# Four engine queues held to the written order of a streaming-encoder trunk

## The chip, the cores and the metric

The kernel runs on one core of a Trainium2 chip. The metric is the device time of one execution in microseconds (us). Each compute engine (PE for matrix products, DVE, ACT, POOL) works off its own instruction queue, and SP issues nearly all transfers. Instructions of different engines wait for each other through semaphores.

## The reference

One layer over 2,048 tokens of width 1,024, followed by a final norm:

```python
h = rmsnorm(x, norm_g)
c_b, c_c, c_h, c_z, q, k, v, a_z = split(h @ w_in)          # 8 groups of 512 columns
y_c = c_b * causal_dwconv(c_c * c_h, conv_w, conv_b)        # 3 taps
# stick-breaking attention, 8 heads of 64:
z = q @ k.T / 8
rem = reverse exclusive cumsum of log_sigmoid(-z)           # over s < t
y_a = where(s < t, exp(log_sigmoid(z) + rem), 0) @ v
y = group_rmsnorm(concat(y_c, y_a)) * silu(concat(c_z, a_z))
x = x + y @ w_out
x = x + sigmoid(rmsnorm(x) @ w_pg + b_pg) * (p @ w_pe)
return rmsnorm(x, final_g)
```

All of it is in float32, and the outputs are float32.

## The kernel before

**Tiles.** x lies transposed, in four chunks of 512 tokens, which are worked off as c = 3, 2, 1, 0; the pair (3, 2) is called E and the pair (1, 0) L. A projection tile is 128 output columns by 512 tokens. Each factor is split into a high and a low part (`wh`/`wl` for weights, `hhh`/`hhl` for activations; ACT makes the high part, DVE or POOL the low part by a subtraction), and one k-step of 128 is three products on PE (L276, L277, L278). Eight k-steps fill one PSUM tile `pp`. There are two such tiles (tag `mm`), so PE may start the next tile but one only when the evacuation of a tile has run on DVE (L338 for q and k, L388 for gates, L725 and L824 in the last part).

**Attention.** It is worked off in units of (head, query chunk, key chunk). Each unit has four rows. `row_z` makes two matmuls (L527, L528) into one of two `z` tiles, from which ACT takes `s` (L530) and `b` (L532). `row_scan` makes a scan T over s on DVE (L546, L549), POOL copies its last column as the carry (L553), and b times T is taken on DVE or POOL (L555). PE transposes the result (L594), ACT and DVE split it into `ah` and `al` (L597, L602), and two matmuls multiply it by v into `av` (L565, L566), of which there is a single tile. When a head's last unit is through, ACT copies one half of `av` (`tmp`, L574) and DVE adds the other (`ya`, L575); only then is the `av` tile free for the next head.

**Through DRAM.** q, k and v go through DRAM. `evac_qk` takes a tile of q and k from PSUM (DVE L338), makes `sh` (ACT L339) and `sl` (POOL L340), and two steps later issues five stores on SP (L345). `fetch_units` issues the loads of `q` (L509), `kk` (L513) and `vv` (L515) on SP as soon as the stores are recorded as issued, and the four `z` rows of that unit follow in the attention's code.

**Interleaving.** The projections are generators, and `run` goes through them a k-step at a time. After each step it adds a rate to `owed` and pulls that many pieces from the attention's generator. `later` puts off a piece of work by some steps, and `tick` counts them. The order in which the Python code emits instructions is called the written order here. Between it and the queues stands the tile framework's scheduler, which lists each engine's instructions in an order of its own at compile time, with an estimate of what will be ready when.

**Names in the rows.** `gg28_3` is the gate tile of column block 28 and chunk 3; `r2_3` are the norm factors of y for chunk 3, written in code far behind but made from `rg`, which POOL makes (L445) after a power (L439); `rr` is a chunk's norm factor, which PE spreads by a transpose (`rT`, L188); `g3_4` is a tile of the last gate; `z24`, `z72`, `z96`, `z120`, `z144` are the first rows of their units.

Of the kernel before, what the change touches and what calls it, by code (L numbers as in the profile page):

```python
# [28 lines left out]
LAG = 1  # L29

AHEAD = 2


def build(tc, xt_d, pt_d, wst_d, wpe_d, cst_d, out_d):
# [5 lines left out]
    with ctx:  # L40
# [458 lines left out]
        def fetch_units(upto):  # L499

            while got[0] <= min(upto, len(units) - 1):
                n = got[0]
                h, qc, kc = units[n]
                if not all((h, c) in s for c in (qc, kc) for s in (have_qk, have_v)):
                    return
                if kc == qc:
                    q = [att.tile([P, CH], F32R, tag=f"q{i}", bufs=2, name=f"q{i}_{h}_{qc}") for i in (1, 2)]
                    for i in range(2):
                        nc.sync.dma_start(q[i].bitcast(F32),  # L509
                                          qk_d[h][qc][i:i + 2].rearrange("a p t -> (a p) t"))  # L510
                    Q[h, qc] = q
                K[n] = att.tile([P, CH], F32R, tag="kk", bufs=4, name=f"kk{h}_{qc}_{kc}")
                nc.sync.dma_start(K[n].bitcast(F32), qk_d[h][kc][3:5].rearrange("a p t -> (a p) t"))  # L513
                V[n] = att.tile([P, 4, P], F32R, tag="vv", bufs=5, name=f"vv{h}_{qc}_{kc}")
                nc.sync.dma_start(V[n].bitcast(F32).rearrange("p a b -> p (a b)"), v_d[h][kc])  # L515
                got[0] += 1
# [92 lines left out]
        def attention():  # L609

            rows, z = {}, {}
            total = 4 * len(units)
            slots = turns()

            def slot():
                nonlocal slots
                if next(slots, "end") == "end":
                    slots = turns()
                    return next(slots, "end") != "end"
                return True  # L620

            for r in range(total):
                n, j = divmod(r, 4)
                while r not in z:
                    fetch_units(n + AHEAD)
                    if got[0] > n:
                        z[r] = row_z(r)
                    else:
                        yield False
                if j == 0:  # L630
                    fetch_units(n + AHEAD)
                if r + 1 < total and got[0] > (r + 1) // 4:
                    z[r + 1] = row_z(r + 1)
                product_of_row = row_scan(r, *z[r])
                rows.setdefault(n, []).append(z.pop(r))
                yield True
                if j == LAG and n:
                    unit = rows.pop(n - 1)
                    tiles_in_line.extend((n - 1, unit, i) for i in range(4))
                if slot():  # L640
                    yield True
                product_of_row()
                if slot():
                    yield True
            unit = rows.pop(total // 4 - 1)
            tiles_in_line.extend((total // 4 - 1, unit, i) for i in range(4))
            while slot():
                yield True
            while behind:
                weigh(*behind.pop(0))  # L650
                yield True
# [238 lines left out]

        cE, cL = (3, 2), (1, 0)
        stream = attention()
        owed = [0.0]

        def pull():
            return next(stream, None)
# [233 lines left out]
```

## Time and profile before

| | |
|---|---|
| time, median of three runs (lowest, highest) | 1666.65 us (1658.98, 1668.19) |
| the profiled execution's own time | 1666.16 us |
| its span in the trace | 1664.4 us |
| mean granted clock of PE | 0.981 |
| busy: PE, DVE, ACT, POOL | 96%, 68%, 47%, 44% |
| transferred | 334 MB, 201 GB/s on average |

The busy share of PE counts matmuls whose ends are modelled, and it counts a matmul at the lower of the two clock levels (1.2 and 2.4 GHz; a granted clock of 1.00 in the tables is 2.4) as busy for longer. So the time that PE loses in a stretch has two parts: the idle time beside the busy time, and the share by which the granted clock lies under 1.00. The time of the run outside the span is 1.8 us.

### The profile page before, as it was taken

The page shows a single profiled execution, that of the slowest core. Times are in us where ns is not written, and L with a number is a line of the kernel's source. Part 1 is how long each engine was busy: PE and PEld are TensorE (multiplying, and loading weights), DVE is VectorE, ACT ScalarE, POOL GpSimd, SP SyncE. Part 2 cuts the span into 40 slices and gives each one's busy share as a digit, 9 for nine tenths or more (in the row PEclk, how much of TensorE's full clock was granted, in tenths as well). Part 3 has the DMA queues.
Part 4 walks back from the last instruction along what each step waited for, and adds up shares of the span by engine and source line. Part 5 has one row for each costly group of instructions (what it writes and reads, how often), then busy time and mean ns, then how long its engine had stood idle before and what let it go on. Part 6 is the DMA issues. An engine that isn't in the chain of part 4 may idle for free. (4 is left out here: it accounts for less than half of the span.)

```text
span 1664.4 us, 23193 instructions
## 1 busy us (share of the span) xinstructions
PE 1596.0 (96%) x7602; PEld 1289.8 (77%) x7602; DVE 1129.0 (68%) x1473; ACT 782.0 (47%) x1540; POOL 726.6 (44%) x711
## 2 busy tenths in 40 slices
PE   8899999999999999999999999998999999999996
PEld 6687878888878788888888888776767887777875
DVE  7475675856745767777787787789787987334544
ACT  4344453544424545454554444456555554223453
POOL 6434444454360423232433323587574444325541
PEclk9999999999999999999999999999899999999998
DMA  5766765748547646475753433478677856888832
GB/s 178 240 215 201 229 215 184 246 135 272 176 157 226 187 151 173 133 226 152 234 165 114 133 108 121 135 266 286 224 245 259 309 188 215 270 305 285 268 112 84
DMA packets 184712, 333.99 MB, mean 201 GB/s; under 512 B 21776, under 2 KB 22800, under 8 KB 184592
## 3 DMA queue, kind: packets, MB, share of 16 engines
q1 hardware_dynamic: 181712, 327.27, 61.0%
q10 hardware_dynamic: 2880, 5.24, 0.9%
q8 instruction: 60, 0.98, 0.3%
q14 instruction: 60, 0.49, 0.1%
HBM read 217.08 MB, written 115.34 MB: 200 GB/s over the span
## 5 line engine op out<-in xcount | busy, mean ns | idle before, releaser
L276 PE MATMUL pp<-hhh,wh 128*128 128x512 f32 x1008 | 408.5, 405 | 4.7 <-DVE gg L388 3.1
L277 PE MATMUL pp<-hhl,wh 128*128 128x512 f32 x1008 | 403.1, 400 | 3.1 <-DVE hhl L155 3.0
L278 PE MATMUL pp<-hhh,wl 128*128 128x512 f32 x1008 | 400.7, 398 | 0.0
L549 DVE TENSOR_TENSOR_SCAN T<-s,carry,small 128x513 f32<-128x513 f32 x192 | 282.4, 1471 | 111.4 <-ACT s L530 104.6
L530 ACT ACTIVATE s<-z 128x512 f32<-128x512 f32 (+1 forms) x320 | 172.0, 538 | 310.6 <-PE z L528 302.7
L555 POOL TENSOR_TENSOR b<-b,T 128x512 f32<-128x512 f32 (+2 forms) x160 | 177.0, 1106 | 172.3 <-DVE T L549 96.3
L263 POOL TENSOR_TENSOR wl<-wr,wh 128x512 fp32r<-128x512 f32 x126 | 178.2, 1414 | 131.2 <-ACT wh L262 117.9
L277 PEld LDWEIGHTS pp<-hhl,wh 128*128 128x128 f32 x1008 | 192.5, 191 | 43.6 <-DVE hhl L155 8.0
L276 PEld LDWEIGHTS pp<-hhh,wh 128*128 128x128 f32 x1008 | 193.0, 192 | 42.3 <-DVE gg L388 3.5
L278 PEld LDWEIGHTS pp<-hhh,wl 128*128 128x128 f32 x1008 | 192.5, 191 | 42.6
L602 DVE TENSOR_TENSOR al<-tp,ah 128x512 fp32r<-128x512 f32 (+1 forms) x320 | 191.5, 599 | 43.8 <-ACT ah L597 43.0
L597 ACT CAST ah<-tp 128x512 fp32r<-128x512 f32 (+1 forms) x320 | 168.3, 526 | 62.5 <-PE tp L594 58.4
L553 POOL COPY carry<-T 128x1 f32<-128x1 f32 x192 | 54.7, 286 | 322.5 <-DVE T L549 170.0
L594 PE MATMUL tp<-first,b 128*128 128x128 f32 x1088 | 174.3, 274 | 9.9 <-POOL b L555 6.2
L594 PEld LDWEIGHTS tp<-first,b 128*128 128x128 f32 x1088 | 137.5, 141 | 52.6 <-POOL b L555 8.2
L532 ACT ACTIVATE b<-z 128x512 f32<-128x512 f32 (+1 forms) x320 | 170.2, 532 | 0.0
L546 DVE TENSOR_TENSOR_SCAN T<-s,first 128x513 f32<-128x513 f32 (+3 forms) x128 | 118.4, 931 | 62.1 <-ACT s L530 61.9
L565 PE MATMUL av<-ah,vv 128*128 128x512 f32 (+1 forms) x320 | 140.5, 439 | 7.3 <-DVE ya L575 7.3
L555 DVE TENSOR_TENSOR b<-b,T 128x512 f32<-128x512 f32 (+1 forms) x160 | 125.9, 787 | 11.8 <-ACT wh L262 0.5
L527 PE MATMUL z<-kk,q 128*128 128x512 f32 (+1 forms) x320 | 120.6, 377 | 4.4 <-DMA kk<-qk_d 2.3
L262 ACT CAST wh<-wr 128x512 fp32r<-128x512 f32 x126 | 78.2, 622 | 96.8 <-DMA wr<-in_wst_dram 41.5
L566 PE MATMUL av<-al,vv 128*128 128x512 f32 (+1 forms) x320 | 118.7, 371 | 2.5 <-DVE al L602 2.5
(156 smaller groups left out, 2623.0 us busy)
## 6 DMA issues: line engine op xcount, KB each, us to landing
wr<-in_wst_dram SPq DMA_DIRECT2D x128, 256.0 KB, 3.0
wh<-wp_d SPq DMA_DIRECT2D x128, 256.0 KB, 3.3
wl<-wp_d SPq DMA_DIRECT2D x128, 256.0 KB, 3.6
wp_d<-wh SPq DMA_DIRECT2D x94, 256.0 KB, 3.5
wp_d<-wl SPq DMA_DIRECT2D x94, 256.0 KB, 3.6
kk<-qk_d SPq DMA_DIRECT2D x80, 256.0 KB, 4.5
vv<-v_d SPq DMA_DIRECT2D x80, 256.0 KB, 3.8
q<-qk_d SPq DMA_DIRECT2D x64, 256.0 KB, 4.3
```

The costliest lines, as they stand in the source:

```text
L263: nc.gpsimd.tensor_tensor(out=wl, in0=raw, in1=wh.bitcast(F32), op=ALU.subtract)
L276: nc.tensor.matmul(pp, wh[:, sl], hh, start=(kt == 0), stop=False)
L277: nc.tensor.matmul(pp, wh[:, sl], hl, start=False, stop=False)
L278: nc.tensor.matmul(pp, wl[:, sl], hh, start=False, stop=(kt == KT - 1))
L530: nc.scalar.activation(s[:, 1:w + 1], zp[:, 0:w], AF.Sigmoid, scale=-0.125)
L532: nc.scalar.activation(bt[:, 0:w], zp[:, 0:w], AF.Sigmoid, scale=0.125)
L549: nc.vector.tensor_tensor_scan(T[:, 0:w + 1], s[:, 0:w + 1], zeros.to_broadcast([P, w + 1]), carries[h, qc][:, j:j + 1], op0=ALU.mult, op1 ...
L555: return lambda: eng.tensor_tensor(out=bt[:, 0:w], in0=bt[:, 0:w], in1=T[:, 0:w], op=ALU.mult)
L565: nc.tensor.matmul(av[:, 0:w], v[:, kb], ah[:, 0:w], start=diag and kb == 3, stop=False)
L594: nc.tensor.transpose(tp[:, j * P:(j + 1) * P], bt[:, kb * P - k0:(kb + 1) * P - k0], ident)
L597: nc.scalar.copy(ah[:, 0:w], tp[:, 0:w])
L602: nc.vector.tensor_tensor(out=al[:, 0:w], in0=tp[:, 0:w], in1=ah[:, 0:w].bitcast(F32), op=ALU.subtract)
```

## The change

A new function goes through the instructions as they were written, after the whole kernel has been recorded, and ties each instruction of DVE, PE, ACT and POOL to the one written before it on the same engine. The tie is an ordering for the scheduler, with no semaphore. SP is not in the list. Beside that, `owed` begins at -5 rather than 0, so the attention's pieces stand five pulls later among the projection steps, from the start on. No instruction is added or removed on a compute engine.

```diff
--- before.py
+++ after.py
@@ -29,6 +29,19 @@
 LAG = 1
 
 AHEAD = 2
+
+
+def in_line(tc, engines):
+
+    last = {}
+    for ins in list(tc.nc.cur_bb.bb.instructions):
+        if ins.engine in engines:
+            if ins.engine in last:
+                tc.add_manual_dep(
+                    ins, last[ins.engine].name,
+                    mybir.DependencyInfo(mybir.DependencyClass.NoSync, mybir.DependencyReason.DATA),
+                    reason="in_line")
+            last[ins.engine] = ins
 
 
 def build(tc, xt_d, pt_d, wst_d, wpe_d, cst_d, out_d):
@@ -890,7 +903,7 @@
 
         cE, cL = (3, 2), (1, 0)
         stream = attention()
-        owed = [0.0]
+        owed = [-5.0]
 
         def pull():
             return next(stream, None)
@@ -1124,6 +1137,7 @@
     args.append(nc.dram_tensor("out_0_dram", (4, KT, P, CH), F32, kind="ExternalOutput").ap())
     with tile.TileContext(nc) as tc:
         build(tc, *args)
+        in_line(tc, [mybir.EngineType.DVE, mybir.EngineType.PE, mybir.EngineType.Activation, mybir.EngineType.Pool])
     r = run_bass_kernel_spmd(nc, [arrays], core_ids=[0])
     out = r.results[0]["out_0_dram"]
     return np.ascontiguousarray(out.transpose(0, 3, 1, 2).reshape(SEQ, DM)[::-1]).reshape(1, SEQ, DM)
```

Below are three places in the queues; lines behind L31 have numbers greater by 13 in the changed file, so L276 to L278 there are L289 to L291, L527 is L540, L388 is L401, L549 is L562, L575 is L588 and L824 is L837.

PE, in the chunks L, where q and k of head 0 in chunk 1 (`pp16_1`) are ready and the rows of the first unit of the L chunks begin (`z96`). First before:

```order
L276 MATMUL pp17_1_5919<-hhh1_1_5508,wh17_68_5719 128x512
L277 MATMUL pp17_1_5919<-hhl1_1_5509,wh17_68_5719 128x512
L278 MATMUL pp17_1_5919<-hhh1_1_5508,wl17_68_5720 128x512
L276 MATMUL pp17_1_5919<-hhh1_2_5514,wh17_68_5719 128x512
L277 MATMUL pp17_1_5919<-hhl1_2_5515,wh17_68_5719 128x512
L527 MATMUL z96_5791<-kk0_1_1_5779,q1_0_1_5775 128x512
L528 MATMUL z96_5791<-kk0_1_1_5779,q2_0_1_5776 128x512
L527 MATMUL z97_5797<-kk0_1_1_5779,q1_0_1_5775 128x384
```

Then the same unit in the changed kernel:

```order
L289 MATMUL pp16_1_5718<-hhh1_7_5558,wh16_67_5700 128x512
L290 MATMUL pp16_1_5718<-hhl1_7_5559,wh16_67_5700 128x512
L291 MATMUL pp16_1_5718<-hhh1_7_5558,wl16_67_5701 128x512
L289 MATMUL pp16_0_5766<-hhh0_0_5597,wh16_66_5584 128x512
L290 MATMUL pp16_0_5766<-hhl0_0_5598,wh16_66_5584 128x512
L291 MATMUL pp16_0_5766<-hhh0_0_5597,wl16_66_5585 128x512
L540 MATMUL z96_5791<-kk0_1_1_5779,q1_0_1_5775 128x512
L541 MATMUL z96_5791<-kk0_1_1_5779,q2_0_1_5776 128x512
```

`z96` stood 59 rows behind the last product of `pp16_1` before (rows 2277 and 2337 of the queue, with products of `pp17_1` ahead of it); now three products lie between the two. In the same way `z24` and `z72` move up by 16 rows, `z120` by 10 and `z144` by 23. Of PE's 7,267 rows 6,572 keep their number. SP issues the loads of these units in nearly the same places of its own queue, behind the stores of the same tile.

DVE, at the gates of the attention's heads 0 and 1, chunk 3, before:

```order
L437 TENSOR_TENSOR gr3_2_5226<-gs3_2_5221,rr_460 128x32
L438 TENSOR_SCALAR gr3_2_5226<-gr3_2_5226 128x32
L602 TENSOR_TENSOR al22_1_5238<-tp22_1_5234,ah22_1_5237 128x256
L443 TENSOR_SCALAR gr7_3_5248<-gs7_3_5243 128x8
L668 CAST r2_3_11250<-rg_461 128x4x16
L669 TENSOR_TENSOR r2_3_11250<-rg_461,r2_3_11250 128x4x16
L388 TENSOR_TENSOR gg28_3_5262<-pp28_3_5180,rB3_738 128x512
L393 SCALAR_TENSOR_TENSOR gg28_3_5262<-gg28_3_5262,cst_439,sg28_3_5263 128x512
```

And now:

```order
L615 TENSOR_TENSOR al22_2_5195<-tp22_2_5190,ah22_2_5194 128x384
L562 SCALAR_TENSOR_TENSOR T95_5216<-s2_473,carry7_2_4918,small_448 128x513
L450 TENSOR_TENSOR gr3_2_5226<-gs3_2_5221,rr_460 128x32
L451 TENSOR_SCALAR gr3_2_5226<-gr3_2_5226 128x32
L456 TENSOR_SCALAR gr7_3_5248<-gs7_3_5243 128x8
L615 TENSOR_TENSOR al22_1_5238<-tp22_1_5234,ah22_1_5237 128x256
L401 TENSOR_TENSOR gg28_3_5262<-pp28_3_5180,rB3_738 128x512
L406 SCALAR_TENSOR_TENSOR gg28_3_5262<-gg28_3_5262,cst_439,sg28_3_5263 128x512
```

The two instructions that make `r2_3` stand 540 rows further behind now, at rows 981 and 982 of DVE's queue, and the evacuation of `gg28_3` no longer has them ahead of it.

DVE, in the last third, where the final gate (`g3_4`) runs beside the attention of heads 4 and 5 (`ya2_0`), before:

```order
L549 SCALAR_TENSOR_TENSOR T278_13107<-s2_473,carry5_0_12825,small_448 128x513
L555 TENSOR_TENSOR b278_13056<-b278_13056,T278_13107 128x512
L602 TENSOR_TENSOR al68_3_13072<-tp68_3_13066,ah68_3_13071 128x512
L686 TENSOR_TENSOR yt2_5_12964<-yt2_5_12964,gT2_5_13083 128x512
L824 TENSOR_TENSOR g3_4_13086<-px144_3_12942,rB7_12505 128x512
L549 SCALAR_TENSOR_TENSOR T279_13152<-s0_471,carry5_0_12825,small_448 128x513
L830 TENSOR_TENSOR g3_4_13086<-g3_4_13086,e3_4_13021 128x512
L693 TENSOR_TENSOR yhl2_5_13115<-yt2_5_12964,yhh2_5_13114 128x512
L602 TENSOR_TENSOR al68_2_13124<-tp68_2_13119,ah68_2_13123 128x384
L575 TENSOR_TENSOR ya2_0_13128<-av4_0_12407,tmp4_0_13129 64x512
```

And now:

```order
L562 SCALAR_TENSOR_TENSOR T277_13058<-s1_472,carry5_0_12825,small_448 128x513
L699 TENSOR_TENSOR yt2_5_12964<-yt2_5_12964,gT2_5_13083 128x512
L837 TENSOR_TENSOR g3_4_13086<-px144_3_12942,rB7_12505 128x512
L615 TENSOR_TENSOR al68_3_13072<-tp68_3_13066,ah68_3_13071 128x512
L562 SCALAR_TENSOR_TENSOR T278_13107<-s2_473,carry5_0_12825,small_448 128x513
L843 TENSOR_TENSOR g3_4_13086<-g3_4_13086,e3_4_13021 128x512
L588 TENSOR_TENSOR ya2_0_13128<-av4_0_12407,tmp4_0_13129 64x512
L568 TENSOR_TENSOR b278_13056<-b278_13056,T278_13107 128x512
L615 TENSOR_TENSOR al68_2_13124<-tp68_2_13119,ah68_2_13123 128x384
```

The evacuation of `g3_4` (L824, now L837) has moved ahead of two attention rows (`al68_3` and the scan `T278`) and the product of b278, and `ya2_0` (L575, now L588) ahead of that product, of `al68_2`, and of `yhl2_5`. On DVE, 206 of 1,470 rows keep their number; evacuations stand four to five rows earlier on average.

On ACT two changes of that kind lie near the start: `vo0_2`, `vo1_2` and `sh1_3` (L364, L339) stood behind the first unit's `s` and `b` rows and stand ahead of them now.

## Rows read from the trace of the kernel before

**Rows 1.** The page, part 1: busy time and share of each engine.

```profile
PE 1596.0 (96%) x7602; PEld 1289.8 (77%) x7602; DVE 1129.0 (68%) x1473; ACT 782.0 (47%) x1540; POOL 726.6 (44%) x711
```

**Rows 2.** Waits of PE: total us, times, longest us.

```profile
PE av L565 <- DVE ya L575: 7.3, 3, 3.3
...
PE rT L188 <- POOL rr L178: 5.4, 3, 2.8
...
PE gs L428 <- ACT sq L421: 3.5, 3, 2.7
PE pp L276 <- DVE gg L388: 3.1, 1, 3.1
```

**Rows 3.** Busy time by stretch; columns PE, PEld, DVE, ACT, POOL, granted clock, DMA.

```profile
240.00:260.00 20.00, 17.31 (x70) 13.97 (x69) 12.87 (x17) 8.35 (x16) 9.44 (x7) 0.83 0.63 204
...
470.00:500.00 30.00, 26.90 (x116) 21.90 (x115) 8.38 (x14) 4.80 (x8) 15.42 (x10) 0.94 0.50 168
...
545.00:562.00 17.00, 13.79 (x51) 10.00 (x49) 12.07 (x14) 8.36 (x19) 7.69 (x11) 0.80 0.38 124
1095.00:1295.00 200.00, 183.56 (x853) 143.54 (x852) 166.53 (x183) 115.30 (x228) 134.13 (x121) 0.96 0.77 257
```

**Rows 4.** Timeline, 153 to 159 us: start, duration, engine, line; first z row is z24.

```profile
153.88 0.47 SPq L513 DMA_DIRECT2D kk<-qk_d  x1
...
155.28 0.40 PE L278 MATMUL pp<-hhh,wl 128*128 128x512 f32 x1
...
158.34 0.47 PE L527 MATMUL z<-kk,q 128*128 128x512 f32 x1
```

**Rows 5.** Timeline, 535 to 547 us: from the end of pp16_1 to z96.

```profile
535.55 0.40 PE L278 MATMUL pp<-hhh,wl 128*128 128x512 f32 x1
...
536.76 1.29 POOL L340 TENSOR_TENSOR sl<-qk,sh 128x512 fp32r<-128x512 f32 x1 [40.69 <-ACT sh L339]
...
541.88 1.34 SPq L513 DMA_DIRECT2D kk<-qk_d  x3
...
546.56 0.47 PE L527 MATMUL z<-kk,q 128*128 128x512 f32 x1 [0.32 <-DMA kk<-qk_d]
```

**Rows 6.** Timeline, 622 to 626 us (z120) and 709 to 715 us (z144).

```profile
622.74 0.39 PE L278 MATMUL pp<-hhh,wl 128*128 128x512 f32 x1
...
625.48 0.50 PE L527 MATMUL z<-kk,q 128*128 128x512 f32 x1 [0.53 <-DMA kk<-qk_d]
...
709.31 0.39 PE L278 MATMUL pp<-hhh,wl 128*128 128x512 f32 x1
...
714.64 0.50 PE L527 MATMUL z<-kk,q 128*128 128x512 f32 x1 [0.60 <-DMA kk<-qk_d]
```

**Rows 7.** Timeline, 59 to 72 us, ACT: the first s row, and sh1_3.

```profile
59.25 0.60 ACT L530 ACTIVATE s<-z 128x512 f32<-128x512 f32 x1 [1.62 <-PE z L528]
...
71.40 0.62 ACT L339 CAST sh<-qk 128x512 fp32r<-128x512 f32 x1 [2.92 <-DMA v_d<-vo]
```

**Rows 8.** Timeline, 478 to 481 us: rg on POOL, then gg28_3 on DVE.

```profile
478.69 1.64 POOL L445 TENSOR_TENSOR rg<-gr,small 128x8 f32<-128x8 f32 x1
...
480.73 0.68 DVE L388 TENSOR_TENSOR gg<-pp,rB 128x512 f32<-128x512 f32 x1
```

**Rows 9.** Timeline, 1230 to 1235 us, DVE: g3_4 and ya2_0.

```profile
1230.80 0.68 DVE L824 TENSOR_TENSOR g<-px,rB 128x512 f32<-128x512 f32 x1
...
1234.91 0.67 DVE L575 TENSOR_TENSOR ya<-av,tmp 64x512 f32<-64x512 f32 x1
```

**Rows 10.** DVE groups, 1095 to 1295 us: busy us, mean ns, idle before, releasers.

```profile
L549 DVE TENSOR_TENSOR_SCAN T<-s,carry,small 128x513 f32<-128x513 f32 x35 | 59.0, 1686 | 15.1 <-ACT s L530 12.9 <-POOL b L555 2.1
...
L693 DVE TENSOR_TENSOR yhl<-yt,yhh 128x512 fp32r<-128x512 f32 x8 | 11.1, 1384 | 5.1 <-ACT yhh L691 5.0
L155 DVE SCALAR_TENSOR_TENSOR x1hl<-xr,cst,x1hh 128x512 fp32r<-128x512 f32 x9 | 10.3, 1147 | 2.2 <-ACT x1hh L152 2.2
...
L830 DVE TENSOR_TENSOR g<-g,e 128x512 f32<-128x512 f32 x8 | 5.4, 681 | 2.6 <-ACT g L825 2.6
```

## The prediction

> **What bounds the kernel now.** I began with the page's busy shares: PE is busy for 96% of the span and DVE for 68% [rows 1]. The reader should see that no other engine is near full, and so ask where PE's remaining time goes. Two things are in it. The first is waiting, and the list of PE's waits puts names to it: on `ya` 7.3 us in 3 waits, on a norm factor 5.4, on `sq` 3.5, once 3.1 on a gate tile [rows 2]. No single name carries the loss; it is made of a few short clusters. The second is the clock, which I read in the table by stretch. Around a wait of 2.7 us the granted clock is 0.83 for 20 us, so 3.4 us are lost there beside 2.7 of idleness; around the 3.1 us wait it is 0.94 for 30 us, which is 1.8 us [rows 2, 3]. I therefore price a PE wait of near 3 us or more at its length plus 1.8 to 3.4, and take 2.5.
>
> The clusters that the change touches cost, as idle time plus clock: 2.7 + 3.4 = 6.1 us at 240 to 260; 3.1 + 1.8 = 4.9 at 470 to 500; 3.2 + 3.4 = 6.6 at 545 to 562; and 16.4 + 0.04 x 200 = 24.4 from 1095 to 1295 [rows 3]. Then I laid the two orders of each engine beside the timeline and asked of each moved row: what was ready when, and what stands behind it now?
>
> **First part: z rows that can no longer be put off.** The scheduler had moved the first z rows of some units back until their loads had landed. Written order puts them where the code emits them, right behind the issue of those loads, and PE's whole queue stands behind them. Five units are hit. (1) `z24` now follows a product that started at 155.28, so PE gets to it at about 155.5; its kk load was issued at 153.88 and it ran at 158.34 [rows 4]: a stall of 2.8 us. (2) `z72`, of head 6, repeats this with the same 16 rows of displacement: 2.8. (3) `z96` follows three products behind the end of `pp16_1`. The third began at 535.55, so PE arrives at 535.8; but `sl` was made only at 536.76 to 538.05, the kk load issued at 541.88, and z ran at 546.56, having waited for that load [rows 5]: 10.8. (4) `z120` follows the product of 622.74, arrives at 623.0, and had its data at 625.48: 2.5. (5) `z144` follows that of 709.31, arrives at 709.5, and ran at 714.64: 5.1 [rows 6]. The last three waited for kk where they stood, so their data cannot have been there earlier; for the first two, the distance from the issue of kk to z (4.46) is about that of `z96` (4.68), which speaks for the same. The sum is 24.0 us. The bounds: nothing, if the loads were issued as much earlier as PE is; against that, each load hangs on the tile's own evacuation and stores, which hang on PE. Above, 30, if the stores come later on a fuller DVE. I take 24.0, and 1.0 for the unit's next rows, whose `b` are late by the same chain.
>
> **The clock after them.** Three stalls are new at places where PE ran at full clock: `z24`, `z72`, `z144`, at 2.5 each 7.5 us. `z96` brings one too, 3.4, taken from the cluster that it replaces. `z120` is shorter than any stall that I saw followed by a drop, and I count nothing. That a wait of 2.7 us is followed by a granted clock of 0.83 is what the rows show [rows 2, 3]. The Trainium skill, "TensorE: Matmul & The Clock Gate", section "HAM oscillation", gives an abstract rule of how long a gap must be, by which gaps as short as those of `z24` and `z72` would be harmless; by it the forecast would be 5.0 us lower. The trace doesn't bear the rule out as it stands, so the rows decide.
>
> **The start.** `rr` for chunk 2 stands behind two more DVE rows, so the 2.8 us wait for `rT` [rows 2] grows by about 2. `s0` and its fellows ran from 59.25; `vo0_2`, `vo1_2` and `sh1_3` now stand ahead of them, and `sh1_3` ran at 71.40 [rows 7]. At worst the first unit is 12 us late; but the product that `sh1_3` needs moves forward with it, other products fill much of PE, and the five pulls that `owed` holds back make the attention due later anyway. Between -5 (the waits of before vanish) and +12 I take +3, nearer the lower end for these reasons.
>
> **Second part: what written order frees.** (a) At 478, `gg28_3` waited behind the hoisted `r2_3` copies, which waited for POOL's `rg` until 480.33; it ran at 480.73 [rows 8]. Those copies go 540 rows back, so the 4.9 us are gone. They wait there for nothing, since `rg` is long made. (b) At 246, `ya1_3` stood behind sums for the next chunk's norm; it is now eight rows earlier, and the 6.1 us go. (c) The cluster at 545 to 562 came from chain delays around `z96`; with PE stopped ahead of them, DVE and ACT catch up, and I count the 6.6 as gone, against the 10.8 + 3.4 above. (d) From 1095 to 1295 evacuations ran late behind scans: `g3_4` was evacuated at 1230.80, behind two attention rows that it now precedes, and `ya2_0` came at 1234.91 and held PE's next head [rows 9]. Both come earlier now. Of the 24.4 us I take three quarters, 18.3, since DVE is busy for 166.5 of the 200 us there [rows 3] and must idle more in written order. All of it would be 24.4, none of it 0; beside the third rival below this is the widest term.
>
> **The sum.** 24.0 + 1.0 + 7.5 + 3.4 + 3 - 4.9 - 6.1 - 6.6 - 18.3 = +3.0. On the profiled execution's own 1666.16 us (span 1664.4 and 1.8 outside) this gives 1669; the median of the runs shown is 1666.65, so the profiled one is typical. A change under 0.5%, 8 us, can hardly be told from none in this kernel. Everything else I count as nothing: between the named places PE's products cover evacuations that have a whole tile, eight steps, to run, and SP's queue changes little.
>
> **The rivals.**
> *A, faster, 1650.* Written order removes all of the late cluster (6.1 more), the start gains 5 instead of losing 3 (8 less), and the clock holds through `z24` and `z72` (5.0 less): 1669 - 19 = 1650. For it: scans wait on `s` for 12.9 us there [rows 10], so DVE still has time to give. Against it: in the waits of before PE stands still with products behind that have their data [rows 2], so it won't get past a z whose load is in flight, and A has to win it all elsewhere. Where the loads also landed earlier, it would go to 1640.
> *B, slower, 1687.* DVE becomes the bound from 1095 to 1295. The forecast leaves it 181.7 us for 166.5 of work, so 15.2 of idleness. In written order each `x1hl`, `yhl` and gate sum waits for an ACT step made from the DVE row shortly ahead of it; 9 + 8 + 8 of them [rows 10], at ACT's 0.6 us [rows 7], are 15.0, just what it has. The deciding point is there: a further 0.5 us on each of the 35 scans of the second form is 17.5 us, which takes nearly the whole gain, so 1669 + 18.3 = 1687, and 1696 with the start at its worst. Against it: these waits already stand at 5.1, 2.2 and 2.6 in part. For it: a scan already takes 1686 ns here [rows 10], beside a POOL that is busy for 134 of 200 us [rows 3].
> *C, nothing changes, 1666.* 6,572 of PE's rows keep their number; but on DVE 206 of 1,470 do, which all but excludes it.
>
> **Chances.** The forecast 0.36, A 0.32, B 0.29, C 0.03. The forecast's own spread is 1656 to 1682, which puts 0.05 of its 0.36 under 1658 and 0.07 over 1675. With 0.03 of A and 0.03 of B inside 0.5%: faster 0.05 + 0.29 = 0.34, same 0.24 + 0.03 + 0.03 + 0.03 = 0.33, slower 0.07 + 0.26 = 0.33. The range goes from A's far end to B's, 1640 to 1694.
>
> **What would show it.** In the profile after: waits of z for DMA kk near 24 us in all, with one near 10.8; granted clock under 1.00 at `z24`, `z72`, `z144`; no wait on a gate tile near 478 and none on `sq` near 246; PE busy in the stretch of `ya2_0` above 94%. I am wrong if z waits stay short (A), or if DVE's waits on ACT grow and PE's waits move to DVE in the last third (B), or if a wait stands at a place that I have not named, in which case written order cost something in the steady parts.

## The result, and the profile after

The changed kernel takes 1757.73 us (median of three runs, 1751.83 to 1761.82): 1.0556 times the time before, with a 95% interval of 1.0486 to 1.0626. I had forecast 1669 us and a range up to 1694, so the result lies 64 us above it. The profiled execution took 1751.83 us, the fastest of the three; its span is 1750.1 us, 85.7 more than before.

The page of the changed kernel, its span, part 1, and the clock row of part 2 (40 slices):

```profile
span 1750.1 us, 22774 instructions
PE 1605.2 (92%) x7602; PEld 1301.5 (74%) x7602; DVE 1150.0 (66%) x1473; ACT 777.8 (44%) x1540; POOL 765.2 (44%) x711
PEclk8899999989999899999998999989989999999998
```

PE's busy time grew by 9 us against [rows 1] and the span by 86. So some 76 us are new idle time of PE. The other 9 are the same 7,602 instructions taking longer, more of them at the lower clock: 0.961 on average in place of 0.981. The list of PE's waits in the changed kernel (total, times, longest, us), beside [rows 2], says who is waited for:

```profile
PE z L540 <- DMA kk<-qk_d: 29.2, 5, 10.5
PE z L540 <- ACT b L545: 19.7, 3, 11.2
PE gs L441 <- POOL ssc L428: 14.5, 3, 8.7
PE ssp L183 <- DVE acc L233: 9.8, 2, 5.7
PE tp L607 <- POOL b L568: 9.8, 8, 2.9
PE ssp L183 <- DVE xsq L221: 8.9, 1, 8.9
PE vp L372 <- DVE vT L366: 5.1, 1, 5.1
```

The first line is the one that the prediction named, near 24 us, and it is 29.2. All the others are new or much grown. Two of them, on `xsq` (8.9) and 11.2 us of those on `b`, lie in the start, for which my sum has +3; the rest have no term in it. The wait on a gate tile and the long one on `sq` of [rows 2] are gone. The timeline of PE gives each long wait a place (start, duration, instruction, and in brackets the idle time ahead of it and what ended it):

```profile
28.40 1.87 PE L183 MATMUL ssp<-small,xsq 128*128 128x2 f32 x8 [8.88 <-DVE xsq L221]
68.38 0.58 PE L540 MATMUL z<-kk,q 128*128 128x256 f32 x1 [11.20 <-ACT b L545]
164.48 0.76 PE L540 MATMUL z<-kk,q 128*128 128x512 f32 x1 [4.88 <-DMA kk<-qk_d]
269.86 1.87 PE L183 MATMUL ssp<-small,acc 128*128 128x2 f32 x8 [4.09 <-DVE acc L233]
372.73 1.86 PE L183 MATMUL ssp<-small,acc 128*128 128x2 f32 x8 [5.71 <-DVE acc L233]
403.56 0.77 PE L540 MATMUL z<-kk,q 128*128 128x512 f32 x1 [6.94 <-DMA kk<-qk_d]
560.62 1.11 PE L372 MATMUL vp<-first,vT 128*128 128x128 f32 x4 [5.09 <-DVE vT L366]
584.45 0.77 PE L540 MATMUL z<-kk,q 128*128 128x512 f32 x1 [10.51 <-DMA kk<-qk_d]
668.62 0.50 PE L540 MATMUL z<-kk,q 128*128 128x512 f32 x1 [1.79 <-DMA kk<-qk_d]
759.80 0.80 PE L540 MATMUL z<-kk,q 128*128 128x512 f32 x1 [5.11 <-DMA kk<-qk_d]
936.08 0.80 PE L540 MATMUL z<-kk,q 128*128 128x512 f32 x1 [8.09 <-ACT b L545]
1155.56 1.87 PE L441 MATMUL gs<-small,ssc 128*128 128x8 f32 x8 [8.70 <-POOL ssc L428]
```

The five waits for kk are `z24`, `z72`, `z96`, `z120` and `z144`. To see what each place cost on the whole, I took from each trace the start of the n-th of the 4,608 projection products on PE and subtracted that of the kernel before. This is worked out from the traces, in us. Each column is a single execution, so a few us are scatter: that of e2 took 1688.09 us, 6 above its median.

| n-th product | before, at | changed | written order on PE only (e2) | four kinds of rows mended (e15) |
|---|---|---|---|---|
| 288 | 119.3 | +2.0 | -1.8 | +0.2 |
| 432 | 162.7 | +10.5 | +0.7 | -0.3 |
| 720 | 260.9 | +3.4 | +2.6 | -5.3 |
| 1008 | 354.6 | +10.3 | +2.9 | -1.0 |
| 1152 | 401.6 | +26.9 | +8.0 | -1.2 |
| 1728 | 587.4 | +43.7 | +13.3 | +1.0 |
| 2160 | 746.7 | +50.7 | +22.7 | -0.8 |
| 2448 | 851.4 | +50.7 | +22.7 | -1.2 |
| 2592 | 902.5 | +61.0 | +22.7 | -0.9 |
| 3024 | 1056.8 | +61.6 | +22.7 | -0.8 |
| 3168 | 1116.9 | +74.1 | +22.4 | +16.5 |
| 4608 | 1646.0 | +85.8 | +22.1 | +23.9 |

In long stretches nothing is lost: from 746.7 to 851.4 us and from 902.5 to 1056.8 the distance stands still within 0.6 us. The loss comes in jumps at single places up to 1056.8 us, 61.6 in all, and as 24.2 more in the last third, where I had expected 18.3 back.

### The profile page after: what moved, and what is told of

Same layout as the page of the kernel before. It is cut to its first block, busy times and chain, and to the rows that moved or that the text cites. A ratio compares the mean times of both kernels' runs of the same rounds, so it can differ in the third digit from the quotient of the medians.

```text
span 1750.1 us, 22774 instructions
## 1 busy us (share of the span) xinstructions
PE 1605.2 (92%) x7602; PEld 1301.5 (74%) x7602; DVE 1150.0 (66%) x1473; ACT 777.8 (44%) x1540; POOL 765.2 (44%) x711
## 5 line engine op out<-in xcount | busy, mean ns | idle before, releaser
L289 PE MATMUL pp<-hhh,wh 128*128 128x512 f32 x1008 | 409.7, 406 | 0.0
L291 PE MATMUL pp<-hhh,wl 128*128 128x512 f32 x1008 | 400.6, 397 | 0.0
L562 DVE TENSOR_TENSOR_SCAN T<-s,carry,small 128x513 f32<-128x513 f32 x192 | 298.1, 1553 | 0.0
L568 POOL TENSOR_TENSOR b<-b,T 128x512 f32<-128x512 f32 (+2 forms) x160 | 195.7, 1223 | 131.8 <-DVE T L562 64.8
L276 POOL TENSOR_TENSOR wl<-wr,wh 128x512 fp32r<-128x512 f32 x126 | 180.2, 1433 | 123.8 <-ACT wh L275 105.2
L291 PEld LDWEIGHTS pp<-hhh,wl 128*128 128x128 f32 x1008 | 192.5, 191 | 43.6
L289 PEld LDWEIGHTS pp<-hhh,wh 128*128 128x128 f32 x1008 | 193.5, 192 | 36.8 <-issue 1.2
L566 POOL COPY carry<-T 128x1 f32<-128x1 f32 x192 | 66.7, 347 | 298.9 <-DVE T L562 157.2
L607 PE MATMUL tp<-first,b 128*128 128x128 f32 x1088 | 178.3, 278 | 17.6 <-POOL b L568 9.8
L607 PEld LDWEIGHTS tp<-first,b 128*128 128x128 f32 x1088 | 140.9, 144 | 62.2 <-POOL b L568 12.2
L540 PE MATMUL z<-kk,q 128*128 128x512 f32 (+1 forms) x320 | 121.9, 381 | 48.9 <-DMA kk<-qk_d 29.2
L559 DVE TENSOR_TENSOR_SCAN T<-s,first 128x513 f32<-128x513 f32 (+3 forms) x128 | 136.7, 1069 | 40.0 <-ACT s L543 38.9
L568 DVE TENSOR_TENSOR b<-b,T 128x512 f32<-128x512 f32 (+1 forms) x160 | 135.4, 846 | 3.5
L541 PE MATMUL z<-kk,q 128*128 128x512 f32 (+1 forms) x320 | 120.7, 377 | 0.0
L579 PE MATMUL av<-al,vv 128*128 128x512 f32 (+1 forms) x320 | 119.3, 373 | 0.8 <-DVE al L615 0.8
```

The lines of the kernel that those rows point to most:

```text
L276: nc.gpsimd.tensor_tensor(out=wl, in0=raw, in1=wh.bitcast(F32), op=ALU.subtract)
L289: nc.tensor.matmul(pp, wh[:, sl], hh, start=(kt == 0), stop=False)
L291: nc.tensor.matmul(pp, wl[:, sl], hh, start=False, stop=(kt == KT - 1))
L562: nc.vector.tensor_tensor_scan(T[:, 0:w + 1], s[:, 0:w + 1], zeros.to_broadcast([P, w + 1]), carries[h, qc][:, j:j + 1], op0=ALU.mult, op1 ...
L568: return lambda: eng.tensor_tensor(out=bt[:, 0:w], in0=bt[:, 0:w], in1=T[:, 0:w], op=ALU.mult)
L607: nc.tensor.transpose(tp[:, j * P:(j + 1) * P], bt[:, kb * P - k0:(kb + 1) * P - k0], ident)
```

## The experiments

Each time below is a median, with the ratio to runs of the kernel before on the same chip and its 95% interval.

**Which engine?** `in_line` takes a list of engines, so the first runs shorten it. e1 leaves PE out, e2 has PE alone.

```diff
-        in_line(tc, [mybir.EngineType.DVE, mybir.EngineType.PE, mybir.EngineType.Activation, mybir.EngineType.Pool])
+        in_line(tc, [mybir.EngineType.DVE, mybir.EngineType.Activation, mybir.EngineType.Pool])   # e1
+        in_line(tc, [mybir.EngineType.PE])                                                        # e2
```

> Written order for DVE, ACT and POOL only, owed at -5; PE's order is left to the scheduler. If PE's own order carries the loss (its rows moved up into waits, above all z behind its load), nearly all of the 91 us come back: 1660 to 1690 us, and PE's waits on the kk loads fall from 29 us to under 5. If the loss is in the queues of the engines that PE waits for, the waits on sums, on ssc, on xsq and on b stay and the time is 1700 to 1760.

> Written order for PE only, owed at -5. If PE's own order carries the loss: 1735 to 1760 us. If the other queues carry most of it: the z waits alone, 24 to 30 us, with some 8 us of clock, so 1690 to 1710 us.

e1: 1718.55 us, 1.0321 (1.0293 to 1.0349). e2: 1681.74 us, 1.0101 (1.0071 to 1.0132). PE's own order, the theory that I started from, is the smaller part: e1, which is without it, waits 2.9 us on kk and still 9.0 on ssc, 6.9 on `acc` and 6.0 on `b`. Its waits in e2 are those on kk and little else that is new:

```profile
PE z L540 <- DMA kk<-qk_d: 31.9, 8, 10.2
PE av L578 <- DVE ya L588: 7.5, 3, 3.8
PE ssp L183 <- DVE acc L720: 6.2, 2, 4.4
```

e2 was expected at 1690 to 1710 by the theory that the other queues carry most; it came 8 us under that, on the side of that theory.

**The five pulls.** e3 drops the call of `in_line` and keeps `owed` at -5; e4 keeps the call and sets `owed` to -1. The tied program with `owed` at 0 wasn't tried.

> owed at -5 and no written order on any engine. If the tie to the written order carries the loss, the time is that of before within 10 us (1655 to 1677). If the attention's later start carries a part of it, 1680 us or more.

> Written order on all four engines, owed at -1 rather than -5. If the five pulls matter little beside the order: 1740 to 1775 us. If the later start is what collides with the stores and the side work: under 1720 us.

e3: 1657.81 us, 0.9962 (0.9944 to 0.998). e4: 1758.33 us, 1.0559 (1.0531 to 1.0586). So the later start of the attention by itself gains about 0.4%, and under the written order -1 and -5 give the same time. The loss is the order's.

**One engine at a time,** `owed` at -5: DVE (e5), ACT (e6), POOL (e7).

> Written order on DVE alone, owed at -5. Written order on DVE, ACT and POOL together took 1718.6 us. If DVE is the queue that does it (sums for a norm behind gate evacuations, the splits of x ahead of an evacuation): 1690 to 1715 us, with PE's waits on acc, xsq and vT as in the changed kernel. If ACT does it: 1655 to 1675.

> Written order on ACT alone, owed at -5. If ACT is the queue that does it (sh of the start ahead of the first b, and the split of the small gate weights, which waits for stores, ahead of s and b): 1690 to 1715 us with waits of z on b of 8 to 11 us. If DVE does it: 1665 to 1680, those two waits alone being 19 us less what PE can do meanwhile.

> Written order on POOL alone, owed at -5. POOL's rows hardly moved past anything that waits long; both theories: 1655 to 1672 us. More would mean that the sums for the group norms (ssc) wait on POOL's own queue.

e5: 1693.44 us, 1.0196 (1.0161 to 1.0232). e6: 1693.07, 1.0196 (1.0155 to 1.0236). e7: 1724.57, 1.0379 (1.0342 to 1.0416). DVE and ACT each ended in the range that I had given for "this is the queue that does it", at the same time, so neither is the one. The waits that I had named stand in e5 in part (8.1 us on `acc`, 3.5 on `xsq`); in e6 the waits of `z` on `b` are 5.8 us in all, and none is of 8 to 11. For POOL alone both of my theories were wrong by over 50 us. Counted from e3 (0.9962), PE costs 0.0139, DVE 0.0234, ACT 0.0234 and POOL 0.0417, together 0.1024; all four at once cost 0.0594. The effects don't add. One reason can be read from the lists: the wait of `gs` on ssc stands in e6 (8.9 us), in e7 (18.9) and in the changed kernel (14.5), and it can be lost only once. Whether that is the whole reason isn't shown. The waits of PE in e7:

```profile
PE gs L441 <- POOL ssc L428: 18.9, 4, 9.0
PE tp L607 <- POOL b L568: 14.1, 11, 3.1
PE av L578 <- DVE ya L588: 8.8, 3, 4.8
```

Why POOL in particular suffers when it is alone was not pursued further, and no run leaves out POOL alone.

**Distance in the written order.** e8 keeps the written order of all four engines, and writes a unit's first `z` rows only 12 steps behind the issue of its loads:

```diff
-                    if got[0] > n:
+                    if got[0] > n and step[0] - asked[n] >= 12:
                         z[r] = row_z(r)
```

> The changed kernel, with one rule more: a unit's z rows are written only 12 steps or more behind the issue of its loads. If PE's loss on z is only a matter of how few rows the code writes between a load and its use, the 29 us of z waiting for kk go to under 5 us and some 8 us of clock come back: 1715 to 1728 us. If the wait only moves to the next row that is late (the rival), the time stays above 1740.

e8: 1719.64 us, 1.0322 (1.0297 to 1.0348). As expected: z waits once more for kk, 3.2 us, and 38 us come back. e9 moves the other named rows as well:

```diff
-            later(2, norm_r, c, acc)
+            later(8, norm_r, c, acc)
-                later(4, group_r, 3, c, ssc[c], 8, blk8)
+                later(10, group_r, 3, c, ssc[c], 8, blk8)
-            later(5, group_r, 4 + pr, c, sq, 2, blk2)
+            later(9, group_r, 4 + pr, c, sq, 2, blk2)
...
                 nc.sync.dma_start(we_d[m], t.bitcast(F32))
+                yield
+                yield
...
-                    if chunks == cL and (kind, i) in (("g", 0), ("g", 1)):
-                        b = (pairs_e,) * 2
+                    if chunks == cL and (kind, i) in (("g", 0), ("g", 1), ("g", 2)):
+                        b = (nodrain(pairs_e), nodrain(pairs_e))   # eight pieces per tile, no rest at the end
```

> As the last, and besides the sums of a chunk's norm are read 8 steps (2 before) behind the last square, the group sums 10 and 9 steps (4 and 5 before), and the eight small gate weights are split over three gate projections in place of two, with two more steps behind each store. If distance in the written order is what was missing: the waits on acc (9.8 us), ssc (14.5) and b at 936 (8.1) go too, 1670 to 1695 us. If written order costs in the steady stretches as well, 1700 or more.

> The last kernel without the rule for z: only the sums and the small gate weights are moved. By the theory of distance 1715 to 1735 us, z waiting for kk staying at 25 to 30 us; and the sum of this gain and that of the run on z alone near the gain of both together.

e9: 1701.09 us, 1.0216 (1.0199 to 1.0233). e10, which is e9 without the rule for z: 1733.41, 1.041 (1.0379 to 1.0442). The gains from 1757.7 are 38 (e8), 24 (e10) and 57 (e9), which nearly add. e9 ends at the number that the expectation gave to the other theory, that the steady stretches cost something too. Its trace doesn't say so: at 1056.8 us it is 8.6 behind the kernel before, and the other 28.6 come in the last third. The wait on ssc has left its list of PE's waits, and that on `acc` of the chunk's squares is down from 9.8 to 1.2 us. It loses 14.4 between 448.6 and 529.2 us and gets 7.0 of these back by 587.4. The wait on `vT` (5.2 us), which no rule moved, is in that stretch, and a new one, at 480, that comes from POOL's queue. The timeline of e9:

```profile
473.48 5.87 POOL L455 TENSOR_TENSOR gr<-gr,small 128x32 f32<-128x32 f32 x1
479.44 0.24 POOL L456 TENSOR_TENSOR rg<-gr,rr 128x32 f32<-128x32 f32 x1
479.63 0.46 POOL L573 TENSOR_TENSOR b<-b,T 128x128 f32<-128x128 f32 x1
480.14 0.47 PE L612 MATMUL tp<-first,b 128*128 128x128 f32 x1 [4.81 <-POOL b L573]
```

With the sum put off, the power of 5.87 us is put off too, and now stands ahead of a product b that the transposes wait for. The wait moved to a neighbour.

**What is gained by the one good move?** e11 has no written order; it ties only the two copies of `r2` behind the DVE instruction written ahead of them, with `owed` at -5.

```diff
+            tied.append(len(tc.nc.cur_bb.bb.instructions))      # in y_prep, ahead of the copies
+    for n in tied:
+        dve = [i for i in body[:n] if i.engine == mybir.EngineType.DVE]
+        after = [i for i in body[n:n + 20] if i.engine == mybir.EngineType.DVE]
+        tc.add_manual_dep(after[0], dve[-1].name, ..., reason="tie")
```

> No written order; owed at -5, and only the copies of the factors r2 (L668 in the kernel before) are tied behind the DVE instruction that is written before them. owed at -5 alone took 0.9962 of before. If the wait on the gate tile near 478 is caused by those copies alone, it goes, and its clock drop with it: 3 to 5 us less, a ratio of 0.992 to 0.995. If another row takes the wait over, 0.996 to 0.998.

e11: 1655.7 us, 0.9942 (0.9928 to 0.9956). It is 0.6% faster than the kernel before. How much of that is the tie the times don't settle, since the interval of e3 (0.9944 to 0.998) overlaps; the traces show it at the place: between 448.6 and 494.1 us e11 gains 5.0 us on the kernel before, and e3 loses 1.2. In the stretch of [rows 3] from 470 to 500, which had 26.90 us busy at 0.94 (and 26.90 at 0.89 in e3), the trace of e11 reads:

```profile
470.00:500.00 30.00, 30.00 (x134) 24.86 (x133) 10.30 (x15) 9.33 (x15) 10.28 (x7) 1.00 0.63 204
```

PE has no idle time there now, and the clock doesn't fall.

**Is the last third's loss its own?** e12 ties only the instructions written ahead of the two last convolution tiles, e13 only those behind.

```diff
-    for ins in list(tc.nc.cur_bb.bb.instructions):
+    body = list(tc.nc.cur_bb.bb.instructions)
+    for ins in body[:tied[0]]:      # e12; e13 has body[tied[0]:]
```

> Written order on all four engines for the instructions written ahead of the two last convolution tiles (up to about 1060 us of the kernel before), the rest left to the scheduler; owed at -5. In the changed kernel the distance to before is 61.6 us at that point and 85.8 at the end. If the two parts are independent: 1664 + 61 = 1720 to 1732 us. If the late loss is a consequence of what the early part does to the state of the queues, nearly all of it stays: 1745 or more.

> The complement: written order only from the two last convolution tiles on. If independent: before plus 18 to 26 us, 1680 to 1692, with a wait of gs on ssc near 9 us at 1100 and waits on yt and b of POOL. If the late part by itself frees evacuations, as the prediction had it, 1640 to 1655.

e12: 1726.31 us, 1.0374 (1.0358 to 1.0389). e13: 1683.42 us, 1.0121 (1.0098 to 1.0144). Both at the independent values. In distances to before: e12 goes from 62.2 at the 3,024th product to 61.1 at the end, e13 from -9.9 to 19.0. (e13's early gain is that of e11, since the `r2` copies are written behind the cut and so are tied.) The last third loses in its own right.

**Squares ahead of the gate.** In the changed kernel the group sum at 1155 waited for ssc, whose square stands behind the gate on ACT and whose addition stands behind the gate's product on POOL. The chain of the changed kernel:

```profile
1149.16 0.69 DVE L706 TENSOR_TENSOR yhl<-yt,yhh 128x512 fp32r<-128x512 f32 x1 [2.36 <-ACT yhh L704]
...
1150.71 0.68 DVE L401 TENSOR_TENSOR gg<-pp,rB 128x512 f32<-128x512 f32 x1
1151.48 0.63 ACT L402 ACTIVATE sg<-gg 128x512 f32<-128x512 f32 x1 [2.35 <-DVE gg L401]
1152.02 0.61 ACT L427 ACTIVATE sq<-cc 128x512 f32<-128x512 f32 x1
...
1152.97 1.31 POOL L420 TENSOR_TENSOR gg<-gg,cc 128x512 f32<-128x512 f32 x1 [4.50 <-DVE gg L406]
...
1154.25 1.26 POOL L428 TENSOR_TENSOR ssc<-ssc,sq 128x512 f32<-128x512 f32 x1
```

Before, this square ran well ahead of the gate. In the order of ACT `sq3_0` stood ten rows ahead of the gate's sigmoid, and now it stands right behind. Its input `cc` doesn't depend on the gate at all. e14 writes the square and its addition ahead of the gate's evacuation; e15 has that, the rule for z, the chunk sums 8 steps behind, and the small gate weights as in e9.

```diff
             def evac(c, pp):
+                if gi < 4:
+                    conv_squares(gi, c)      # square and sum, moved here out of conv_post
                 gg, sg = buf("gg", f"gg{t}_{c}"), buf("sg", f"sg{t}_{c}")
```

> The changed kernel, in which the square of a convolution tile and its sum into ssc are written ahead of the gate's evacuation rather than behind it. If the group sums are late because their squares now queue behind the gate on ACT and POOL: PE's 14.5 us of waits on ssc go and with them some 5 us of clock, 1735 to 1745 us. If the sums are late because the steps behind them hold too few products: no change, 1750 to 1762.

> Written order on all four engines with the rule for z, the chunk sums read 8 steps behind, the small gate weights on three gate projections, and the squares written first in place of later group sums. By the theory that every piece of the loss is a place where written order puts a row behind something late, this is at or under the 1701 us of the kernel with the group sums put off: 1688 to 1702. Not under that of before, since the splits of x at 540 and the last third remain.

e14: 1754.15 us, 1.0548 (1.0531 to 1.0566). That is in the range that I had given for no change. Yet PE's waits on ssc fell from 14.5 to 8.3 us, so the squares' place has a part in them; only the time hardly fell. In its timeline the last of them is 3.1 in place of 8.70 us, and the next matmuls wait for `wl` instead (3.15 us at 1168). e15: 1690.63 us, 1.0165 (1.0142 to 1.0189), within its range and better than e9. Now the table by stretch, split where PE has done some 5,000 of its matmul records, with the columns of [rows 3]. First e15:

```profile
0.00:1057.00 1057.00, 1017.56 (x4981) 838.55 (x4982) 729.42 (x975) 483.67 (x993) 457.61 (x443) 0.98 0.56 181
1057.00:1688.00 631.00, 575.77 (x2623) 453.50 (x2621) 415.87 (x499) 293.11 (x548) 322.75 (x268) 0.97 0.69 227
```

The kernel before, split at the same place:

```profile
0.00:1057.00 1057.00, 1029.01 (x5003) 842.47 (x5004) 718.07 (x987) 492.00 (x1003) 415.03 (x446) 0.99 0.57 182
1057.00:1664.00 607.00, 566.99 (x2600) 447.31 (x2599) 410.93 (x487) 289.99 (x538) 311.56 (x265) 0.97 0.70 234
```

The changed kernel:

```profile
0.00:1119.00 1119.00, 1034.52 (x5005) 853.23 (x5006) 741.15 (x984) 489.91 (x1002) 450.42 (x445) 0.96 0.54 171
1119.00:1750.00 631.00, 570.64 (x2599) 448.25 (x2597) 408.85 (x490) 287.85 (x538) 314.79 (x266) 0.97 0.69 225
```

With four kinds of rows rewritten, the written order is as fast as the kernel before over the first 1,057 us, and the last third still takes 631 us in place of 607. Those 24 us are the same in e15 and in the changed kernel, so the repairs do nothing for them on balance.

## Why the prediction was wrong

**Right: the z rows.** I named five units and 24.0 us; the waits are 4.88, 6.94, 10.51, 1.79 and 5.11, 29.2 in all. `z96` was priced at 10.8. Too low were `z24` and `z72`, at 2.8 each: I had the load of `z24` issued 1.6 us ahead of PE's arrival, and in the changed kernel SP issued it at 159.80, when PE already stood; `z24` ran 4.68 us later. By PE's order alone the distance reaches +22.7 us (in e2, whose traced execution was slower than its median; e3, without any order, stands at -1.1 there); my net for this part, 24.0 + 1.0 + 7.5 + 3.4 - 6.6, was 29.3. The clock fell as forecast, and around the 1.79 us wait of `z120`, as I had it, it did not. The table by stretch of the changed kernel shows `z24`, the wait at 936, and `z120`:

```profile
155.00:175.00 20.00, 15.12 (x72) 12.57 (x71) 9.12 (x13) 6.55 (x16) 5.24 (x5) 0.83 0.71 220
...
925.00:945.00 20.00, 11.91 (x52) 9.55 (x51) 8.48 (x10) 7.18 (x15) 7.50 (x8) 0.74 0.59 194
...
650.00:700.00 50.00, 48.21 (x243) 39.63 (x242) 35.94 (x48) 24.54 (x50) 13.94 (x20) 1.00 0.53 159
```

One caution on that price. 0.83 over 20 us makes 3.4 us at `z24`, but a part of the low clock lies inside the long wait, where no matmul runs. The same table in smaller pieces, the wait and the stretch behind it:

```profile
159.60:164.48 4.88, 0.01 (x1) 0.03 (x1) 0.76 (x2) 0.47 (x2) 0.00 (x0) 0.75 1.03 322
164.48:168.90 4.42, 4.42 (x16) 3.94 (x17) 2.46 (x4) 3.00 (x8) 0.00 (x0) 0.50 0.85 275
168.90:175.00 6.10, 6.10 (x35) 5.12 (x34) 5.21 (x7) 2.81 (x7) 4.25 (x4) 1.00 0.43 126
```

PE works at 0.50 for 4.4 us, so 2.2 are lost, where I had taken 2.5. Over the whole run the two mean clocks would make some 37 us more loss in the changed kernel, and PE's busy time grew by 9. So idle time and the clock's share, added up as in the section on the time before, count some time twice where waits are long.

**Right in sum, by other ways: the start.** +3 was forecast; at the 288th product it is +2.0, with waits of 8.88 and 11.20 us inside, which the kernel before spends in other ways. `s0` came behind `sh1_3` as described.

**Right, and given back: (a) and (b).** Between the 576th product (211.0 us) and the 720th the distance falls from 9.5 to 3.4, the 6.1 us of (b). But of the sums that I had moved out of the way I didn't ask who waits for them. They are the chunk's squares, and `ssp` on PE is next: 4.09 us at 269.86 and 5.71 at 372.73. With the first of the two 6.9 us are lost again by the 864th product. The wait of (a) went, and e11 alone gains the 5.0 us there that I had at 4.9; in the changed kernel `gs` waited 2.4 and 3.3 us for ssc nearby (a part of the 14.5).

**The step that failed:** "Everything else I count as nothing: between the named places PE's products cover evacuations that have a whole tile, eight steps, to run". By the terms of my sum, +21.3 us come up to the last third and -18.3 in it; measured were +61.6 and +24.2. So the miss is 40.3 us of loss that I had at nothing, and 42.5 in (d), below. Of the 40.3, 28.7 are waits without a term (4.09 and 5.71 on `acc`, 2.44 and 3.31 on ssc, 5.09 on `vT`, 8.09 on `b`) and 5.2 the longer z waits; the rest I put down mostly to the clock behind those waits, which isn't shown place by place. I had looked for PE rows that moved, and costed those. In these six waits, what is late is the DVE, ACT or POOL row that PE waits for, and in e1, where PE is left to the scheduler, waits on ssc, `acc` and `b` remain. For `ssp`, `gs` and `vp` only 2 to 5 steps are written between the last producer and the matmul. The scheduler had pulled the producer ahead where its input was there before, as the square `sq3_0` ten rows ahead of the gate's sigmoid shows; for the others this is argued. The place at 936 shows the form that I missed altogether. The timeline of the changed kernel there, PE's `z` and ACT:

```profile
924.85 0.40 PE L541 MATMUL z<-kk,q 128*128 128x512 f32 x1
...
927.68 0.41 ACT L782 CAST wes<-we 128x256 fp32r<-128x256 f32 x1 [3.85 <-DMA we_d<-wes]
931.29 0.40 ACT L782 CAST wes<-we 128x256 fp32r<-128x256 f32 x1 [3.20 <-DMA we_d<-wes]
934.64 0.40 ACT L782 CAST wes<-we 128x256 fp32r<-128x256 f32 x1 [2.94 <-DMA we_d<-wes]
934.95 0.59 ACT L543 ACTIVATE s<-z 128x512 f32<-128x512 f32 x1
```

The small gate weights go through a single buffer, so each split waits for the store of the one before. Their code is emptied at the end of a tile, all that is left of it at once, and what the scheduler had spread over the attention's rows now stands in a lump ahead of `s` and `b`. PE waits 8.09 us. The Trainium skill, "Perfetto Trace Analysis", section "Tensor Engine Instruction", says that ACT and DVE work strictly first in, first out; the trace agrees, since the second matmul of that `z` began at 924.85 and its `s` only at 934.95. The splits of x ahead of `vT` at 560 (5.09 us) are such a lump on DVE. In e15, where the small gate weights are spread out, the wait at 936 is gone; the one on `vT`, which I left as it was, is still there with 5.1 us.

**Wrong in sign: (d).** I counted 18.3 us back from the last third; 24.2 more were lost. In the stretch that I had costed nothing came back and nothing was lost: from the 3,119th product to the 3,523rd (1095.1 to 1295.2 us before, 1172.4 to 1372.2 now) the distance goes from 77.3 to 77.0. The loss lies in front of it (15.7 us, from 61.6 to 77.3) and behind it (8.8). The table by stretch, first the front part before:

```profile
1057.00:1095.10 38.10, 38.10 (x180) 28.36 (x180) 31.69 (x45) 20.58 (x41) 31.85 (x21) 1.00 0.60 195
```

The changed kernel, the front part and then the stretch of (d):

```profile
1118.70:1172.40 53.70, 41.56 (x180) 30.70 (x179) 31.00 (x48) 22.43 (x45) 33.97 (x27) 0.90 0.46 157
...
1172.40:1372.20 199.80, 181.54 (x852) 142.73 (x851) 167.72 (x177) 111.88 (x223) 130.59 (x114) 0.97 0.77 249
```

In front PE had no idle time; now it has 12.1 us, 8.70 of them the wait on ssc. In the stretch of (d) evacuations did move up, and PE's waits on `ya` fell from 7.3 to 2.4 us as I had it; but the transposes now wait 9.1 us for `b` from POOL, a wait that this stretch didn't have. PE is busy for 91% of it (92% before), and not for over 94%, which I had named as a sign. Rival B's sum for the stretch, no gain, came out. That DVE became its bound was not seen: DVE is busy for 84% of it (83% before), and PE's largest new wait there is on POOL. What the runs show is whose order it is. From the 3,024th product to the end the distance grows by 35.7 us with POOL alone (e7), by 11.4 with DVE (e5), by 9.0 with ACT (e6), and by -0.6 with PE (e2). What stays open is the row-by-row cause: mending the group sum at 1155 (e14) shortened that wait, but at the 3,119th product e14 is 78.3 us behind, where the changed kernel is 77.3, so the loss moved to neighbours. That y, the gate and the attention take turns on three engines there, each behind the other's longest chain, is argued from rows like those above and not shown.

**The rivals.** A was wrong, and C was excluded by its own argument. B was nearest, and too low by 70 us, because its price was bounded by the one stretch. (Its own far end was 1696 us; the range stops at 1694.)

## What to carry to other kernels

When a change reorders queues, don't list only the rows that moved on the bound engine; list for each row of the bound engine its producers, and ask of each what stands ahead of it now, on whatever engine. Hold to written order only what the scheduler demonstrably puts in a bad place: one tied pair of copies, with the five pulls (0.9962 by themselves), gave 0.9942, all four engines tied 1.0556. Here the written order came level with the scheduler's over the first 1,057 us once the code itself kept the distance between a producer and its reader, and spread side work rather than emptying it at a tile's end; in the last third that was not enough.

## What the runs showed of the hardware that I had not expected

Holding queues to an order is not additive: four engines singly cost 0.102 of the time, together 0.059, and POOL alone no less than DVE, ACT and POOL together (1.0379 against 1.0321, with intervals that touch). A PE wait that is removed can be paid elsewhere by nearly the same sum: e14 took 6.2 us of waits on ssc away and gained 3.6 us against the median of the changed kernel, which is within the two kernels' intervals. It need not be: in e8 the z waits went, and 38 us came back.
